# Splitting 128x128 fp32 transposes into two 64-row tiles in a streaming encoder step

## The chip, the cores and the metric

The kernel runs on one core of a Trainium2 chip. The metric is device time in microseconds (us) from launch to end; a verdict on a changed kernel comes from timed runs of both kernels on the same chip. The engines of the core are TensorE (in the profile PE for matmuls and PEld for the loads of stationary operands), VectorE (DVE), ScalarE (ACT), GpSimd (POOL) and SyncE (SP, which issues transfers).

## The reference: what is computed

One inference step of a one-layer encoder, for a prompt of 512 frames and a sample of 32 frames of a running stream, in fp32. The input (model width 1024) is normalised and projected by one wide matrix. Two branches follow:

- an mLSTM branch: causal convolution and silu, four heads of width 512 with queries, keys and values, a gated score matrix, a matrix memory, a layer norm per head;
- an HGRN2 branch: eight heads of width 128 with a gated, decaying linear attention, an RMS norm per head and a silu gate.

```python
hm = _head_layernorm(hm.transpose(0, 2, 1, 3), mnorm_g[l].astype(f32))
hm = (hm + m_skip[l].astype(f32) * c) * jax.nn.silu(z_m.astype(f32))
ya = hm.astype(x.dtype) @ w_brm[l]
...
oh = _head_rmsnorm(oh.transpose(0, 2, 1, 3), hnorm_g[l].astype(f32)) * jax.nn.silu(g_h.astype(f32))
yb = oh.astype(x.dtype) @ w_brh[l]
y = jax.nn.sigmoid(ga) * ya + jax.nn.sigmoid(gb) * yb
h = h + y @ w_out[l]
h = h + jax.nn.sigmoid(h @ w_pg[l]) * (p[l] @ w_ple[l])
```

The branches are merged, projected, gated with a per-layer embedding and normalised. Outputs are both streams and all new states (convolution rows, memories, normalisers).

## The kernel before

All activations lie with channels on the 128 partitions and the 544 = 32 + 512 frames along the free dimension. Dense products are written as three products of a high and a low part (fp32r operands), as in `dense` (line 160) and in the classes `One` (line 420) and `Two` (line 477), whose matmuls are lines 460 and 608. `Two` computes two output tiles with seven products of half-size blocks and is the main part of the TensorE work. Such a product's matmul has 272 moving columns.

A `Pump` (line 702) holds the projections still to be done. The attention work of a head is a Python generator: `mchain(h, pump)` for the mLSTM, `chain(h)` (line 1801) for HGRN2. Each `yield n` hands TensorE over to the pump for n half steps, so that the head's own work stands between projection matmuls. TensorE's order is thus written out by hand (`tc.manual_schedule` with the engine PE), and the other engines' order comes from a planner with priorities (`tc.high_priority`) and from `tc.issue_after`. PSUM tiles of the head's work come from `paux` (line 101): two banks of 512 fp32 each, two such tiles in turn; the projections have four single banks from another pool.

Where a head needs another layout, TensorE transposes: `PE.transpose(out, in_, identity)` is a matmul whose stationary operand is the data and whose moving operand is an identity matrix. The places, with the tiles' names in the profile:

- `kt` (line 1122): keys of a head, four blocks of 128 frames, four transposes each; ScalarE then writes the weighted high part (line 1126), VectorE the low part (line 1127). `kts` (line 1135) is the same for the sample, three copies of 32 columns.
- `vt` and `vts` (lines 1157, 1175): the values of heads 1 to 3, with copies in lines 1164, 1165, 1178 and 1182.
- `yt` (lines 1307, 1308): the head's output back to channels on partitions, four blocks of the prompt and one of the sample, for each of four channel tiles per head; VectorE adds it to the skip path in lines 1314 and 1315.
- `pd` (line 1871): five transposes per HGRN2 head, summed along the free dimension by one reduction (line 1873).
- `ht` (lines 1902, 1903): values and keys of a HGRN2 head, five transposes each; ScalarE copies them (lines 1905 to 1909).
- `hoT` (lines 1975, 1976): the HGRN2 head's output, partly with the anti-diagonal `anti` in place of `ident` to turn the order of frames; VectorE multiplies it with the norm's gain and the gate (lines 1979, 1980). The gate itself is made in line 1749.

Other matmuls that use part of the array's rows or columns are the column transposes `cols` (line 916, 4 rows), the broadcasts of the norm (line 248, in part 32 or 16 rows), and the sample's products `nm` (line 1203) and `vq` (line 1586), which have 32 stationary columns.

Of the kernel before, what the change touches and what calls it, by code (L numbers as in the profile page):

```python
# [9 lines left out]
F32 = mybir.dt.float32  # L10
# [16 lines left out]
KH = HD // P  # L27
HH = 8
NB = NP // P
# [7 lines left out]
QUADS = P // NS  # L37
# [25 lines left out]
V_FG, V_CW, V_CB, V_MG, V_SK, V_LB, V_HG, V_CS, V_GV = 0, 8, 72, 88, 104, 120, 136, 144, 192  # L63
# [4 lines left out]
def hybrid_step(ctx: ExitStack, tc: tile.TileContext, a, o):  # L68
    nc = tc.nc
    V, S, G, PE = nc.vector, nc.scalar, nc.gpsimd, nc.tensor  # L70
# [20 lines left out]
    def two(ap):  # L91
        return ap.rearrange("p (a b) -> p a b", a=2)
# [129 lines left out]
    def vcol(i):  # L222
        return vec[:, i : i + 1]
# [888 lines left out]
    def mchain(h, pump):  # L1112
# [5 lines left out]
        for b in range(NB):  # L1118
            yield 4 if h else 1
            pt = paux(f"kt{h}{b}")  # L1120
            for f in range(KH):
                PE.transpose(pt[:, 0, f * P : (f + 1) * P], kf[f][:, NS + b * P : NS + (b + 1) * P], ident)  # L1122
            kh, kl = slot(f"kwh{h}{b}", F32R), slot(f"kwl{h}{b}", F32R)
            wc = col[:, 10 + b, h : h + 1]
            with tc.high_priority():
                kh_ = S.mul(kh[:, :HD], pt[:, 0, :], wc)
                kl_ = V.scalar_tensor_tensor(kl[:, :HD], pt[:, 0, :], wc, kh[:, :HD].bitcast(F32), ALU.mult, ALU.subtract)
            kw.append((kh, kl))
            if h == 0 and b == NB - 2:
                with tc.issue_after(kh_.ins), tc.issue_after(kl_.ins):  # L1130
                    sample_values(vsum)
        yield 4 if h else 2
        pt = paux(f"kts{h}")
        for f in range(KH):
            PE.transpose(pt[: 3 * NS, 0, f * P : (f + 1) * P], ksm[:, f], ident)

        kws = small("kws", [3 * NS, HD], F32R, bufs=1)
        wc = cols[:, 1, h : h + 1]
        with tc.high_priority():
            S.mul(kws, pt[: 3 * NS, 0, :], wc)  # L1140
            lo = slice(2 * NS, 3 * NS)
            low = V.scalar_tensor_tensor(kws[lo], pt[lo, 0, :], wc[lo], kws[lo].bitcast(F32), ALU.mult, ALU.subtract)
# [4 lines left out]
        if h == 0:  # L1147
            vv, vs = t["vv"], t["vs"]
        else:
            yield max(0, max(pump.when["v", f] for f in range(KH)) - pump.done)  # L1150
            vt = t["vt"]
            vv = []
            for b in range(NB):
                yield 1
                pt = paux(f"vt{h}{b}")
                for f in range(KH):
                    PE.transpose(pt[:, 0, f * P : (f + 1) * P], vt[f][:, NS + b * P : NS + (b + 1) * P], ident)
                if b < 2:
                    vhl = sp.tile([P, 2, SLOT], F32R, tag="d", name=f"vhl{h}{b}", bufs=2)
                    vh, vl = vhl[:, 0], vhl[:, 1]  # L1160
                else:
                    vh, vl = slot(f"vh{h}{b}", F32R), slot(f"vl{h}{b}", F32R)
                with tc.high_priority():
                    S.copy(vh[:, :HD], pt[:, 0, :])
                    V.tensor_tensor(vl[:, :HD], pt[:, 0, :], vh[:, :HD].bitcast(F32), ALU.subtract)
                G.tensor_copy(vh[:, HD:VW], one4)
                filled = G.tensor_copy(vl[:, HD:VW], zero4)
                vv.append((vh, vl))
            yield 1
            pt = paux(f"vts{h}")  # L1170
            vsm, copied = triple(vt, "vsm", t["copied"])
            with tc.issue_after(filled.ins):
                make_late(3 if h < MH - 1 else 2, copied)
            for f in range(KH):
                PE.transpose(pt[: 3 * NS, 0, f * P : (f + 1) * P], vsm[:, f], ident)
            vs = small("vs", [3 * NS, VW], F32R, bufs=1)
            with tc.high_priority():
                S.copy(vs[:, :HD], pt[: 3 * NS, 0, :])
            G.tensor_copy(vs[:, HD:VW], vone)
            lo = slice(NS, 2 * NS)  # L1180
            with tc.high_priority():
                low = V.tensor_tensor(vs[lo, :HD], pt[lo, 0, :], vs[lo, :HD].bitcast(F32), ALU.subtract)
        yield 3

        def new_memory(f, g):
# [113 lines left out]
        for f in range(KH):  # L1299
            while parts:  # L1300
                yield 4
                new_memory(*parts.pop(0))
            yield max(GAP - (16 if h == MH - 1 else 0 if h else 4) if f == 0 else 1 if h else 2, pump.when["z", f] - pump.done)
            ft = h * KH + f
            pt = paux(f"yt{ft}")
            for b in range(NB):
                PE.transpose(pt[:, 0, b * P : (b + 1) * P], yb[b][:, f * P : (f + 1) * P], ident)
# [388 lines left out]
    def units():  # L1696
# [104 lines left out]
    def chain(h):  # L1801
# [10 lines left out]
        for li, c in enumerate(LEVELS):  # L1812
# [53 lines left out]
            if li == 0:  # L1866

                yield 1
                pn = paux(f"pd{h}")
                for b, c_ in enumerate([c_ for c_, _, _ in chunks] + [slice(NA, NA + P)]):  # L1870
                    PE.transpose(pn[:, b // NB, b % NB * P : (b % NB + 1) * P], kq[:, c_], ident)
                with tc.high_priority():
                    V.tensor_reduce(
                        dg, pn.rearrange("p a t -> p (a t)")[:, : 5 * P].rearrange("p (b t) -> p b t", t=P), AX.X, ALU.add
                    )
            if li == (4 if h < HH - 1 else 6) and h:
                yield 1
                finish(h - 1)
# [19 lines left out]
        for n, src, dst, dss in ((0, ii, it, its), (2, kk, kt, kts)):  # L1898
            yield n
            pt = paux(f"ht{h}")  # L1900
            for b, (c, _, _) in enumerate(chunks):
                PE.transpose(pt[:, 0, b * P : (b + 1) * P], src[:, c], ident)  # L1902
            PE.transpose(pt[:, 1, :P], quads(src, n // 2), ident)
            with tc.high_priority():
                S.copy(dst, pt[:, 0, :])
                if n:
                    S.mul(dss, pt[:, 1, :P], 1.0 / QUADS)
                else:
                    S.copy(dss, pt[:, 1, :P])
# [60 lines left out]
    def finish(h):  # L1970

        ov, osb, gg = (hs[h][k] for k in ("ov", "osb", "gg"))
        pt = paux(f"hoT{h}")
        for b, (_, _, j) in enumerate(chunks):
            PE.transpose(pt[:, 0, b * P : (b + 1) * P], ov[:, b * P : (b + 1) * P], ident if j else anti)
        PE.transpose(pt[:, 1, :P], osb, anti)
        g = vcol(V_HG + h)
        ob = slot(f"ob{h}")
        V.scalar_tensor_tensor(ob[:, NS:T], pt[:, 0, :], g, gg[:, NS:T], ALU.mult, ALU.mult)
# [315 lines left out]
```

## Time and profile before

| | |
|---|---|
| timed runs, median of 3 | 1104.29 us |
| lowest and highest | 1103.76 and 1106.26 us |
| profiled execution, first to last instruction (span) | 1101.5 us |
| TensorE matmul, busy | 1092.4 us |
| VectorE, busy | 922.8 us |
| ScalarE, busy | 693.1 us |
| GpSimd, busy | 209.5 us |

The profiled execution's own time is known as its span alone, 1101.5 us; the median of the timed runs is 2.8 us longer. In the views below a row names the line of the kernel, the engine, the operation, the tiles as out<-in, and shapes as partitions x elements; for matmuls rows\*columns of the stationary operand stands ahead. A matmul's shown length includes the depth of its pipeline, so the distance of two starts tells its rate, not its length. In the rows of a timeline the first column is the start, the second the length of a group of like instructions, and xN their count.

### The profile page before, as it was taken

What the parts mean: (1) busy time and instruction counts of PE and PEld (TensorE: products, weight loads), DVE (VectorE), ACT (ScalarE), POOL (GpSimd) and SP (SyncE); (2) the same over time, 40 slices, a digit from 0 to 9 for tenths busy, and PEclk for the clock granted to TensorE, in tenths of its full rate; (3) what the DMA queues carried; (4) which work ended last, traced back from release to release, by engine and by line L of the source; (5) the groups of instructions that cost most, each with busy time, mean ns of one, the idle gap of its engine ahead of it and who ended that gap; (6) DMA issues with size and microseconds to landing.
All of it is one profiled execution on the core that took longest, in us unless ns stands there. A gap on an engine that the chain in (4) does not pass through costs nothing.

```text
span 1101.5 us, 23773 instructions
## 1 busy us (share of the span) xinstructions
PE 1092.4 (99%) x8625; PEld 1070.9 (97%) x8625; DVE 922.8 (84%) x2103; ACT 693.1 (63%) x1579; POOL 209.5 (19%) x375
## 2 busy tenths in 40 slices
PE   9999999999999999999999999999999999999997
PEld 9899999999999999999999999999999999999997
DVE  7889988686896786986888799999999977778885
ACT  7777557754666554665656476776776666446683
POOL 5204010303022021202120123232232210000002
PEclk9999999999999999999999999999999999999999
DMA  7135415639355276554798665666765683337753
GB/s 241 50 124 157 156 58 185 158 125 220 119 178 179 93 178 176 164 167 146 212 261 254 172 145 141 144 135 152 159 145 150 155 222 103 110 90 242 247 180 121
DMA packets 97262, 176.58 MB, mean 160 GB/s; under 512 B 11284, under 2 KB 18580, under 8 KB 96888
## 3 DMA queue, kind: packets, MB, share of 16 engines
q1 hardware_dynamic: 81072, 141.01, 39.9%
q0 software_dynamic: 15184, 32.93, 16.2%
q8 instruction: 68, 1.11, 0.4%
q10 hardware_dynamic: 888, 1.12, 0.3%
q14 instruction: 50, 0.41, 0.1%
HBM read 150.10 MB, written 41.69 MB: 174 GB/s over the span
## 4 chain that ended last, share of the span: by engine, by line
PE 93%; DMA 3%; DVE 2%; issue 1%; SPq 0%; ACT 0%; POOL 0%; ACTq 0%; POOLq 0%
PE d L608 44%; PE ya L167 9%; PE yb L167 4%; PE q L167 4%; PE k L167 4%; PE C L1077 4%; PE nm L1257 3%; PE sc L1037 2%; PE pl L1832 2%; PE u L291 2%; PE d L460 2%; PE vp L1576 2%; DMA ws<-in_w_in 1%; PE ple L167 1%; PE kt L1122 1%; PE ht L1902 1%
## 5 line engine op out<-in xcount | busy, mean ns | idle before, releaser
L495 POOL DMA_DIRECT2D ws<-in_w_in x46 | 40.2, 875 | 211.3 <-DVE hkq L1850 32.2
L622 ACT COPY t<-d 128x272 f32<-128x272 f32 x153 | 58.0, 379 | 14.0 <-PE d L608 14.0
L1850 DVE TENSOR_TENSOR hkq<-hkq,q 128x288 f32<-128x288 f32 (+1 forms) x96 | 40.7, 431 | 2.6 <-PE pl L1834 1.0
L785 DVE SCALAR_TENSOR_TENSOR cv<-ub,vec,cv 128x547 f32<-128x547 f32 x48 | 37.6, 784 | 1.6 <-ACT cv L780 1.2
L1832 PE MATMUL pl<-hkq,km 128*128 128x128 f32 x224 | 36.2, 283 | 0.6 <-ACT km L1818 0.5
L1818 ACT COPY km<-hkq 128x256 f32<-128x256 f32 x56 | 23.9, 428 | 14.2 <-DVE hkq L1850 5.2
L1832 PEld LDWEIGHTS pl<-hkq,km 128*128 128x128 f32 x224 | 30.3, 189 | 2.0 <-ACT km L1818 1.5
L1191 DVE SCALAR_TENSOR_TENSOR c<-c,wi,Cs 128x258 f32<-128x258 f32 x32 | 15.3, 479 | 18.8 <-PE Cs L1189 18.5
L1354 DVE TENSOR_TENSOR y<-ya,y 128x272 f32<-128x272 f32 x48 | 18.9, 435 | 12.1 <-PE ya L167 10.3
L1089 ACT COPY Co<-C 128x258 f32<-128x258 f32 x30 | 9.8, 378 | 27.3 <-PE C L1077 24.9
L1857 DVE COPY_PREDICATED at<-lmask,pl 128x256 f32<-128x256 uint8 (+1 forms) x56 | 25.2, 451 | 0.1
L777 POOL COPY uo<-ub 128x3 f32<-128x3 f32 x16 | 18.7, 1167 | 34.5 <-DVE ub L631 26.6
L1268 ACT COPY y<-nm 128x516 f32<-128x516 f32 x16 | 9.4, 590 | 23.0 <-PE nm L1257 22.5
L133 POOL TENSOR_TENSOR wple50l<-wple5r,wple50h 128x256 fp32r<-128x256 f32 x1 | 0.7, 736 | 120.9 <-ACT wple50h L132 120.9
L961 POOL COPY ksm<-kf 128x96 f32<-128x96 f32 x16 | 7.1, 445 | 84.9 <-ACT kf L975 84.9
L961 POOL COPY vsm<-vt 128x96 f32<-128x96 f32 x12 | 6.3, 525 | 85.9 <-ACT vt L633 43.5
L1797 POOL TENSOR_SCALAR_AFFINE_SELECT aa<-at 128x128 f32<-128x128 f32 x32 | 19.6, 643 | 8.2 <-DVE at L1857 8.0
L581 POOL DMA_DIRECT2D ws<-in_w_in x14 | 14.6, 1043 | 33.1 <-DVE ws272l L133 27.3
L1245 DVE BATCH_NORM_STATS2 bs<-y 128x6 f32<-128x512 f32 (+1 forms) x20 | 13.8, 692 | 8.3 <-ACT y L1268 8.0
L1257 PE MATMUL nm<-vhl,sh 128*128 128x258 f32 x112 | 18.4, 286 | 0.0
L376 POOL DMA_DIRECT2D w_pg_d<-in_w_pg x16 | 13.1, 818 | 25.1 <-issue 21.4
L1956 ACT ACTIVATE osq<-kq 128x128 f32<-128x128 f32 x32 | 9.8, 305 | 12.4 <-DVE kq L1951 12.1
(4735 smaller groups left out, 5086.7 us busy)
## 6 DMA issues: line engine op xcount, KB each, us to landing
ws<-in_w_in POOLq DMA_DIRECT2D x60, 256.0 KB, 4.9
ws<-in_w_in SPq DMA_DIRECT2D x46, 256.0 KB, 3.9
ya_d<-y SPq DMA_DIRECT2D x32, 272.0 KB, 2.3
y<-ya_d SPq DMA_DIRECT2D x24, 272.0 KB, 3.3
w_out_d<-in_w_out POOLq DMA_DIRECT2D x24, 256.0 KB, 6.5
w_pg_d<-in_w_pg POOLq DMA_DIRECT2D x24, 256.0 KB, 6.5
c<-in_C SPq DMA_DIRECT2D x16, 258.0 KB, 3.8
out_Cs<-c SPq DMA_DIRECT2D x16, 258.0 KB, 3.8
```

Source lines behind the costliest of these rows:

```text
L167: PE.matmul(both[b][:m, :TH], part(w, off + k * step, m, x), xx[:, half(b)], start=(k == 0 and j == 0), stop=(k == n - 1 and j == 2),)
L291: PE.matmul(both[b][:m, :TH], part(w, off + k * step, m, x), xx[:, half(b)], start=(k == 0 and j == 0), stop=(k == KD - 1 and j == 2),)
L495: G.dma_start(t, piece(u, i), accum_op=ALU.add)
L608: PE.matmul(ps, ww[:, c], xx, start=(start and k == 0 and j == 0), stop=end, skip_group_check=not start,)
L622: self.kept = S.copy(t, ps)
L785: V.scalar_tensor_tensor(cv[:, :547], ub[:, j : j + 547], vcol(V_CW + 4 * ft + j), cv[:, :547], ALU.mult, ALU.add)
L1077: PE.matmul(pn[g][:, :VH], kw[b][x][:, f * P : (f + 1) * P], vv[b][y][:, g * VH : (g + 1) * VH], start=(b == 0 and j == 0), stop=(b == NB ...
L1257: PE.matmul(pn[:, g, :VH], st[j][x][:, (i - j) * P : (i - j + 1) * P], vv[j][y][:, g * VH : (g + 1) * VH], start=(j == 0 and q == 0), stop ...
L1818: low = S.copy(km.rearrange("p (n j c) -> p n j c", j=2, c=c), view(kk, HB, ((2 * c, NA // (2 * c)), (c - HB, 2), (1, c))),)
L1832: PE.matmul(out, km[:, b * P : (b + 1) * P], view(qq, b * P, dims), start=True, stop=True)
L1850: V.tensor_tensor(x, x, d, ALU.mult)
L1857: V.copy_predicated(at[:, :n], lmask[:, li, :n], pn[:, 0, :n])
```

## The change

Every 128x128 transpose becomes two: the first takes the upper 64 rows of the stationary operand (partitions 0 to 63) with a 64x64 piece of the identity, the second the lower 64 rows. Each moves 64 columns, and each writes its 64 result columns into its own PSUM bank of the tile. A transposed block thus lies half in bank 0 and half in bank 1, and all readers go through views (`turned` for the PSUM side, `quarters` for the SBUF side) that put the halves back in order. With kt and kts, yt and hoT, one VectorE instruction becomes two, over half the columns each. The sample parts of yt and hoT become single transposes of 32 rows and 32 moving columns in bank 0. In HGRN2 the norm's gain is multiplied into the gate instead of into the transposed output.

```diff
+    HP = P // 2
+
+    def turn(pt, i, src, eye=None):
+
+        n = src.shape[-1]
+        for r in range(2):
+            k = slice(r * HP, (r + 1) * HP)
+            at_ = ident[k, k] if eye is None else eye[k, P - (r + 1) * HP : P - r * HP]
+            PE.transpose(pt[:n, r, i * HP : (i + 1) * HP], src[k], at_)
+
+    def turned(pt, n, m=P):
+        return pt[:m, :, : n * HP].rearrange("p r (f c) -> p f r c", f=n)
+
+    def quarters(t):
+        return t.rearrange("p (f r c) -> p f r c", r=2, c=HP)
...
-                PE.transpose(pt[:, 0, f * P : (f + 1) * P], kf[f][:, NS + b * P : NS + (b + 1) * P], ident)
+                turn(pt, f, kf[f][:, NS + b * P : NS + (b + 1) * P])
...
-                kh_ = S.mul(kh[:, :HD], pt[:, 0, :], wc)
-                kl_ = V.scalar_tensor_tensor(kl[:, :HD], pt[:, 0, :], wc, kh[:, :HD].bitcast(F32), ALU.mult, ALU.subtract)
+                rows, hi, lo = turned(pt, KH), quarters(kh[:, :HD]), quarters(kl[:, :HD])
+                kh_ = S.mul(hi, rows, wc)
+                for r in range(2):
+                    kl_ = V.scalar_tensor_tensor(
+                        lo[:, :, r], rows[:, :, r], wc, hi[:, :, r].bitcast(F32), ALU.mult, ALU.subtract
+                    )
...
-                PE.transpose(pt[:, 0, b * P : (b + 1) * P], yb[b][:, f * P : (f + 1) * P], ident)
-            PE.transpose(pt[:, 1, :P], yb[NB][:, f * P : (f + 1) * P], ident)
+                turn(pt, b, yb[b][:, f * P : (f + 1) * P])
+            PE.transpose(pt[:, 0, 2 * P : 2 * P + NS], yb[NB][:NS, f * P : (f + 1) * P], ident[:NS, :NS])
...
-                V.scalar_tensor_tensor(c[:, NS:T], pt[:, 0, :], g, c[:, NS:T], ALU.mult, ALU.add)
-                V.scalar_tensor_tensor(c[:, :NS], pt[:, 1, :NS], g, c[:, :NS], ALU.mult, ALU.add)
+                for r in range(2):
+                    cr = quarters(c[:, NS:T])[:, :, r]
+                    V.scalar_tensor_tensor(cr, turned(pt, NB)[:, :, r], g, cr, ALU.mult, ALU.add)
+                V.scalar_tensor_tensor(c[:, :NS], pt[:, 0, 2 * P : 2 * P + NS], g, c[:, :NS], ALU.mult, ALU.add)
...
-            V.tensor_tensor(t[:, :T], t[:, :T], sg[:, :T], ALU.mult)
+            V.scalar_tensor_tensor(t[:, :T], t[:, :T], vcol(V_HG + h), sg[:, :T], ALU.mult, ALU.mult)
...
-                PE.transpose(pt[:, 0, b * P : (b + 1) * P], src[:, c], ident)
-            PE.transpose(pt[:, 1, :P], quads(src, n // 2), ident)
+                turn(pt, b, src[:, c])
+            turn(pt, NB, quads(src, n // 2))
...
-            PE.transpose(pt[:, 0, b * P : (b + 1) * P], ov[:, b * P : (b + 1) * P], ident if j else anti)
-        PE.transpose(pt[:, 1, :P], osb, anti)
+            turn(pt, b, ov[:, b * P : (b + 1) * P], None if j else anti)
+        PE.transpose(pt[:, 0, 2 * P : 2 * P + NS], osb[:NS], anti[:NS, P - NS :])
...
-        V.scalar_tensor_tensor(ob[:, NS:T], pt[:, 0, :], g, gg[:, NS:T], ALU.mult, ALU.mult)
-        V.scalar_tensor_tensor(ob[:, :NS], pt[:, 1, P - NS : P], g, gg[:, :NS], ALU.mult, ALU.mult)
+        V.tensor_tensor(oq[:, :2], rows[:, :2, ::-1], gq[:, :2], ALU.mult)
+        V.tensor_tensor(oq[:, 2:], rows[:, 2:], gq[:, 2:], ALU.mult)
+        V.tensor_tensor(ob[:, :NS], pt[:, 0, 2 * P : 2 * P + NS], gg[:, :NS], ALU.mult)
```

The other places (kts, vt, vts and pd) are rewritten in the same way.

More of the change, by code (lines that the diff above doesn't have):

```diff
@@ L1134, in mchain @@
         for f in range(KH):
-            PE.transpose(pt[: 3 * NS, 0, f * P : (f + 1) * P], ksm[:, f], ident)
+            turn(pt, f, ksm[:, f])
         kws = small("kws", [3 * NS, HD], F32R, bufs=1)
@@ L1139, in mchain @@
         with tc.high_priority():
-            S.mul(kws, pt[: 3 * NS, 0, :], wc)
+            rows, kq = turned(pt, KH, 3 * NS), quarters(kws)
+            S.mul(kq, rows, wc)
             lo = slice(2 * NS, 3 * NS)
-            low = V.scalar_tensor_tensor(kws[lo], pt[lo, 0, :], wc[lo], kws[lo].bitcast(F32), ALU.mult, ALU.subtract)
+            for r in range(2):
+                low = V.scalar_tensor_tensor(
+                    kq[lo, :, r], rows[lo, :, r], wc[lo], kq[lo, :, r].bitcast(F32), ALU.mult, ALU.subtract
+                )
         c0 = [eslot(f"c0{h}{f}") for f in range(KH)]
@@ L1156, in mchain @@
                 for f in range(KH):
-                    PE.transpose(pt[:, 0, f * P : (f + 1) * P], vt[f][:, NS + b * P : NS + (b + 1) * P], ident)
+                    turn(pt, f, vt[f][:, NS + b * P : NS + (b + 1) * P])
                 if b < 2:
@@ L1174, in mchain @@
             for f in range(KH):
-                PE.transpose(pt[: 3 * NS, 0, f * P : (f + 1) * P], vsm[:, f], ident)
+                turn(pt, f, vsm[:, f])
             vs = small("vs", [3 * NS, VW], F32R, bufs=1)
             with tc.high_priority():
-                S.copy(vs[:, :HD], pt[: 3 * NS, 0, :])
+                S.copy(quarters(vs[:, :HD]), turned(pt, KH, 3 * NS))
             G.tensor_copy(vs[:, HD:VW], vone)
@@ L1313, in mchain @@
             with tc.high_priority():
[L1314 to L1315 removed]
+                for r in range(2):
+                    cr = quarters(c[:, NS:T])[:, :, r]
+                    V.scalar_tensor_tensor(cr, turned(pt, NB)[:, :, r], g, cr, ALU.mult, ALU.add)
+                V.scalar_tensor_tensor(c[:, :NS], pt[:, 0, 2 * P : 2 * P + NS], g, c[:, :NS], ALU.mult, ALU.add)
             with nullcontext() if 0 < h < MH - 1 else tc.high_priority():
@@ L1870, in chain @@
                 for b, c_ in enumerate([c_ for c_, _, _ in chunks] + [slice(NA, NA + P)]):
-                    PE.transpose(pn[:, b // NB, b % NB * P : (b % NB + 1) * P], kq[:, c_], ident)
+                    turn(pn, b, kq[:, c_])
                 with tc.high_priority():
-                    V.tensor_reduce(
-                        dg, pn.rearrange("p a t -> p (a t)")[:, : 5 * P].rearrange("p (b t) -> p b t", t=P), AX.X, ALU.add
-                    )
+                    V.tensor_reduce(dg, turned(pn, NB + 1), AX.XY, ALU.add)
             if li == (4 if h < HH - 1 else 6) and h:
```

22 lines of the change are left out of this document (15 added, 7 removed).

## The prediction

> **What bounds the kernel now.** The page is read first, for the engine that sets the span: its head, the busy times, the granted clock, and the chain of work that ended last, by engine.
>
> ```profile
> span 1101.5 us, 23773 instructions
> ...
> PE 1092.4 (99%) x8625; PEld 1070.9 (97%) x8625; DVE 922.8 (84%) x2103; ACT 693.1 (63%) x1579; POOL 209.5 (19%) x375
> ...
> PEclk9999999999999999999999999999999999999999
> ...
> PE 93%; DMA 3%; DVE 2%; issue 1%; SPq 0%; ACT 0%; POOL 0%; ACTq 0%; POOLq 0%
> ```
>
> Then the busy times by stretch: the mLSTM heads are 100 to 600 us, the HGRN2 heads 600 to 870 us.
>
> ```profile
> 100.00:600.00 500.00, 499.45 (x3979) 490.11 (x3978) 401.60 (x862) 300.33 (x639) 90.41 (x184) 1.00 0.58 169
> 600.00:870.00 270.00, 269.33 (x2182) 266.66 (x2181) 255.72 (x690) 184.57 (x502) 70.18 (x101) 1.00 0.64 151
> ```
>
> TensorE stands still for 0.55 us of the first stretch and 0.67 us of the second, at full clock. Whatever TensorE time the change adds or removes there goes to the end one for one. VectorE has 98.4 us free in the first stretch, but only 14.3 us in the second.
>
> The transposes, all in these stretches, by line (duration min/median/max; it includes pipeline depth, so it isn't the rate):
>
> ```profile
> L1122 PE MATMUL kt<-ident,kf x64: 270/272/328, 109.1 to 534.5; 128*128 128x128 f32 x64
> L1135 PE MATMUL kts<-ident,ksm x16: 270/272/273, 115.0 to 538.0; 128*96 128x128 f32 x16
> L1157 PE MATMUL vt<-ident,vt x48: 270/272/316, 250.3 to 550.3; 128*128 128x128 f32 x48
> L1175 PE MATMUL vts<-ident,vsm x12: 272/273/286, 255.2 to 551.6; 128*96 128x128 f32 x12
> L1307 PE MATMUL yt<-ident,y x64: 270/272/300, 153.6 to 584.5; 128*128 128x128 f32 x64
> L1871 PE MATMUL pd<-ident,kq x40: 270/272/273, 629.0 to 843.3; 128*128 128x128 f32 x40
> L1902 PE MATMUL ht<-ident,hi x32: 270/272/299, 647.4 to 862.4; 128*128 128x128 f32 x32
> L1975 PE MATMUL hoT<-anti,kq x16: 270/272/273, 672.4 to 883.0; 128*128 128x128 f32 x16
> ```
>
> They come in short runs between the projections' matmuls: 35 runs of four (kt 16, kts 4, vt 12, vts 3) and 48 of five (yt 16 with line 1308, pd 8, ht 16 with line 1903 and a second source, hoT 8 with line 1976 and ident rows). That is 140 + 240 = 380 transposes; 356 are split and 24 (lines 1308 and 1976) become small 32-row ones.
>
> **What a run costs now.** The first run of kt in order of time, matmuls (PE) and then weight loads (PEld); columns are start, length of the group, count:
>
> ```profile
> 108.89 0.42 PE L460 MATMUL d<-xh,wi340l 128*128 128x272 f32 x2
> 109.15 0.60 PE L1122 MATMUL kt<-ident,kf 128*128 128x128 f32 x4
> 109.50 0.50 PE L460 MATMUL d<-xh,wi340h 128*128 128x272 f32 x2
> ...
> 114.97 0.60 PE L1135 MATMUL kts<-ident,ksm 128*96 128x128 f32 x4
> ```
>
> ```profile
> 109.03 0.48 PEld L1122 LDWEIGHTS kt<-ident,kf 128*128 128x128 f32 x4
> 109.48 0.30 PEld L460 LDWEIGHTS d<-xh,wi340h 128*128 128x128 f32 x2
> 109.72 0.32 PEld L460 LDWEIGHTS d<-xl,wi340h 128*128 128x128 f32 x2
> 109.97 0.19 PEld L460 LDWEIGHTS d<-xh,wi340l 128*128 128x128 f32 x1
> ```
>
> Less the last one's 0.272, kt's group puts its fourth start at 109.48: three steps in 0.33 us, 0.109 each. kts, with 96 weight columns instead of 128, takes the same 0.60 us, so the step is the 128 moving columns (0.85 ns each), with the weight load hidden. The load of the first transpose is issued at 109.03, 0.01 us after the preceding matmul's start (108.89 + 0.42 - 0.29 = 109.02): nothing drains. Behind the run d starts early on paper and slips; its second matmul starts at 109.50 + 0.50 - 0.29 = 109.71, so the first one counts from 109.71 - 0.125 = 109.585, where 0.125 is the step of the loads 109.72 to 109.97 halved. From d to d a run of four takes 0.57 us, one of five 0.68.
>
> **What a change of tile height costs.** The kernel has this already, in two places: 32-row matmuls between 128-row ones. First the small column transposes (4 rows, so in the array's 32-row tiles, and the same kind of fp32 transpose):
>
> ```profile
> 90.73 0.42 PE L167 MATMUL q<-cs3h,wq001l 128*128 128x272 f32 x2
> 91.08 1.19 PEld L916 LDWEIGHTS cols<-ident,row 4*128 4x128 f32 x18 [0.15 <-issue]
> 92.19 0.22 PEld L918 LDWEIGHTS cols<-ident,r 4*96 4x96 f32 x3
> 92.22 0.28 PE L918 MATMUL cols<-ident,r 4*96 4x4 f32 x3
> 92.43 0.52 PE L167 MATMUL q<-cs0h,wq010h 128*128 128x272 f32 x2
> ```
>
> Second, the broadcast of the norm, full-height rows and then one block of 32 rows:
>
> ```profile
> 25.93 0.50 PE L248 MATMUL r0pb<-ident,rms_r 128*128 128x128 f32 x3
> ...
> 26.35 0.29 PEld L248 LDWEIGHTS r0pb<-ident,rms_r 32*128 32x128 f32 x2
> 26.68 0.30 PEld L291 LDWEIGHTS u<-x,wu30h 128*128 128x128 f32 x2
> ```
>
> Going in: the last q starts at 90.73 + 0.42 - 0.29 = 90.86 and streams about 0.115; the load of cols comes at 91.08, some 0.10 after that, where kt's came 0.01 after the start. In the broadcast the last full-height matmul starts at 26.155, streams 128 columns in 0.109, and the 32-row load comes at 26.35, 0.09 later. No work stands between. Going out: the last cols matmul starts at 92.32 and the load of q comes at 92.43, 0.11 later; that load's matmul counts from 92.43 + 0.52 - 0.29 - 0.125 = 92.53. So each switch empties the array, about 0.09 us, and the next load, otherwise hidden, stands open: 0.107 for a plain one (92.53 less 92.43; d's two behind kt are 0.30 - 0.19 = 0.11 apart), and about 0.056 for a transpose, since 18 loads of 128 columns in cols take (1.19 - 0.14) / 17 = 0.062 each, and of 96 columns (0.22 - 0.12) / 2 = 0.05, that is 0.44 ns a column and 0.006.
>
> **The change, part by part.** *A pair of half-height tiles.* Each has a load of 128 columns, 0.062, and 64 moving columns, 0.054. If both tiles work side by side, a pair takes the longer, 0.062; one after the other, 0.124. No two row tiles are at work in the trace; nearest is a row where four column tiles are:
>
> ```profile
> 119.05 0.16 PEld L1203 LDWEIGHTS nm<-c,qw 128*32 128x32 f32 x8
> ```
>
> Eight loads of 32 columns are through within 0.16 us; at the plain load's 0.84 ns a column (0.107 / 128) they would take 0.215 in turn. So loads of different tiles overlap; I take 0.062, saving 0.047 per pair, and keep 0.124 for the range.
>
> *The switch in:* the preceding d streams 0.115, drains 0.095, the first load is open for 0.056: 0.266 from d to the first pair, where it is 109.15 - 109.02 = 0.13 now: +0.137. *The switch out:* last pair 0.054, drain 0.09, d's load 0.107: 0.251, where it is 0.57 - 0.13 - 3 x 0.109 = 0.115 now: +0.136. Between them three steps of 0.062 instead of 0.109: -0.142. Run of four: +0.131. Run of five pairs (pd, ht): +0.083. With 96 columns (kts, vts) a pair takes about 0.057 and the first load 0.042: +0.096.
>
> *yt and hoT* end with a 32-row tile, a second switch inside the run: from the last pair to it 0.054 + 0.09 + 0.056 = 0.200 instead of 0.109, and out of it 0.027 + 0.09 + 0.107 = 0.224 instead of 0.115. With +0.137 and -0.142 this makes +0.194.
>
> Sum on TensorE: 28 x 0.131 + 7 x 0.096 + 24 x 0.083 + 24 x 0.194 = 3.7 + 0.7 + 2.0 + 4.7 = **11.0 us** (3.5 of it in the HGRN2 heads).
>
> Weighed against a page: the four-row loads ran at 0.062 for 128 columns. The Trainium skill, TensorE: Matmul & The Clock Gate, section LDWEIGHTS, gives columns / 1.2 whatever the row count, so 0.107. By it a pair would be no shorter than a whole transpose, and the sum that of the first rival's lower end. The transposes' rows contradict it; q's plain load agrees.
>
> *VectorE.* Two halves replace one scalar_tensor_tensor of 512 columns in kt, kts and yt:
>
> ```profile
> L1127 DVE SCALAR_TENSOR_TENSOR kwl<-kt,col,kwh x16: 737/744/753, 110.9 to 535.7; 128x512 fp32r<-128x512 f32 x16
> L1191 DVE SCALAR_TENSOR_TENSOR c<-c,wi,Cs 128x258 f32<-128x258 f32 x32 | 15.3, 479 | 18.8 <-PE Cs L1189 18.5
> L1979 DVE SCALAR_TENSOR_TENSOR ob<-hoT,vec,hg x8: 739/751/752, 674.1 to 884.2; 128x512 f32<-128x512 f32 x8
> L1850 DVE TENSOR_TENSOR hkq<-hkq,q 128x256 f32<-128x256 f32 x64 | 26.9, 420 | 1.3 <-PE pl L1832 0.5
> ```
>
> 2 x 0.479 - 0.744 = 0.21, for 36 of them 7.7 us, before 600 us, where 98 are free. In hoT 2 x 0.42 - 0.751 = 0.09, 0.7 us in all, and the gate's scale moves into a multiply as long as before or a little longer; the HGRN2 heads' 14.3 us cover this, and TensorE's own 3.5 us add to the cover. ScalarE's copies keep their count and size; no row shows what reading two banks by turns costs, but even a microsecond more for each of the 51 would fit into the 200 and 85 us that ScalarE has free in the two stretches. The cover ends where transposes come close together: the first head's kt runs are 1.2 us apart on two buffers, and one there already waits for the VectorE part. I put 0.4 us for that and for weight splits that come later; bounds 0 and 2. No DMA and no wait on another queue is added or moved.
>
> Total: 1101.5 + 11.0 + 0.4 = 1112.9 us of span. The median of the timed runs stands 2.8 us over the profiled span (1104.29 - 1101.5), so **1115.7 us**.
>
> **Rivals.** *Tiles take turns (slower still).* If the two loads share their path, a pair costs 0.124: +0.378 for four, +0.393 for five, +0.442 for yt and hoT, about 0.29 with 96 columns: 32.6 us. If only the streams take turns, a pair costs 0.109, the run +0.318 or so, with +0.38 for yt and hoT: 27.8 us. Time 1132 to 1137. Against it stand the column tiles' overlapping loads; for it, that those use different columns and here both tiles fill the same ones.
>
> *No emptying between 64- and 128-row tiles (faster).* Then the first load hides behind d as now, d's behind the last pair, and every pair saves 0.047: 356 x 0.047 + 24 x 0.047 = 17.9 us, less 0.4: 1087. It decides if a switch, in and out together, costs less than 3 x 0.047 = 0.14 us. For it: the trace has 32-row switches only. Against it: both kinds of matmul pay there, at each of the four edges shown. The same skill page, Part 3, says that a load is pulled ahead of matmuls in flight if its row group differs; a load for all rows after a 64-row tile has no such free group.
>
> *Half of it.* Only one side of a switch empties the array: the 0.273 of a run falls to about 0.14, what the pairs save: -7 to 0 us, 1097 to 1105.
>
> **How the numbers follow.** The forecast, drains with side-by-side tiles, has 0.58, own range 1112 to 1119 (a pair of 0.056 to 0.07, drains of 0.08 to 0.1, VectorE's 0 to 2 us). Tiles taking turns 0.22, no emptying 0.12, half 0.08. The range of 1103 to 1137 reaches over the upper rival to its bound and leaves out the faster one and part of the half. What this kernel's measurement can tell from no change is about 0.2%, 2.2 us. Faster: 0.12 and 0.03 of the half, 0.15. Same: 0.05 of the half. Slower: 0.80.
>
> **What will show it.** Right: before each run of kt the first load about 0.2 us after the last d's start, not 0.01; d's load 0.14 us behind the last pair; pairs 0.06 apart; TensorE still 99% busy and the span longer in both stretches, with yt and hoT worst. Pairs 0.11 or more apart mean the first rival; first loads that start with the d before them mean the second. I'm wrong altogether if TensorE gets idle time released by VectorE or ScalarE of more than 3 us.

## The result, and the profile after

The changed kernel takes 1113.9 us, median of four runs (1112.96 to 1114.45), beside 1104.03 us for the kernel before on the same chip: ratio 1.0086, 95% interval 1.0071 to 1.0100. It is slower by 9.9 us. The forecast was 1115.7, with 1112 to 1119 as its own range.

The page of the changed kernel, its head and the busy times by engine:

```profile
span 1111.7 us, 24543 instructions
...
PE 1102.7 (99%) x8981; PEld 1064.0 (96%) x8981; DVE 929.2 (84%) x2147; ACT 694.4 (62%) x1579; POOL 203.6 (18%) x375
```

The span grew by 10.2 us and TensorE's busy time by 10.3 (1102.7 less 1092.4). TensorE stands still no longer than before, 9.0 us against 9.1. Busy here is a modelled time: a matmul counts until its result is through, so an array that is being emptied counts as busy (below, the d ahead of kt counts until 108.97 + 0.41 = 109.38, past kt's first start at 109.32). The weight loads show it: there are 356 more of them, their busy time is 6.9 us less (1064.0 against 1070.9), and the load path stands idle for 47.7 us instead of 30.6. The Trainium skill, Perfetto Trace Analysis, section Identifying the Most-Contended Engine, calls the matmul row's busy share no good measure of how close TensorE is to its roofline, and names the busy share of the weight loads, beside the floating-point work done, to use instead. Here the first stayed at 99%, and the second fell from 97% to 96%.

By stretch, in the same columns as the table of before (TensorE, loads, VectorE, ScalarE, GpSimd, clock, DMA share, GB/s):

```profile
100.00:600.00 500.00, 498.56 (x4114) 477.97 (x4113) 401.75 (x887) 293.79 (x627) 81.80 (x184) 1.00 0.57 164
600.00:870.00 270.00, 269.45 (x2297) 261.73 (x2296) 251.45 (x686) 184.99 (x494) 68.78 (x95) 1.00 0.64 155
```

TensorE is idle for 1.44 us of the first stretch (0.55 before) and 0.55 of the second (0.67 before). So with VectorE's 44 further instructions it stands idle for less than a microsecond more, on balance.

The same run of kt as in the prediction, matmuls and then loads of the changed kernel:

```profile
108.97 0.41 PE L476 MATMUL d<-xh,wi340l 128*128 128x272 f32 x2
109.32 0.46 PE L128 MATMUL kt<-ident,kf 64*128 64x64 f32 x8
109.71 0.51 PE L476 MATMUL d<-xh,wi340h 128*128 128x272 f32 x2
```

```profile
109.31 0.33 PEld L128 LDWEIGHTS kt<-ident,kf 64*128 64x128 f32 x8
109.71 0.30 PEld L476 LDWEIGHTS d<-xh,wi340h 128*128 128x128 f32 x2
109.94 0.31 PEld L476 LDWEIGHTS d<-xl,wi340h 128*128 128x128 f32 x2
```

Read as in the prediction: the last d before the run starts at 108.97 + 0.41 - 0.29 = 109.09, and the first load comes 0.22 us later, where it came 0.01 later before. The eight loads span 0.33 us with one load's own 0.13 in it, so three steps from pair to pair take 0.20, 0.067 each by these rounded rows; instruction by instruction the two loads of a pair start 3 to 4 ns apart, and the pairs 0.059 to 0.062. The last pair's matmul starts about 109.71 - 0.15, and the first d behind the run counts from 109.71 + 0.51 - 0.29 - 0.125 = 109.805. From d to d the run takes 0.715 us; it took 0.57.

In the HGRN2 heads, a run of five pairs (pd) and one with a 32-row tile (hoT):

```profile
638.24 0.28 PE L624 MATMUL d<-xfh,ws249l 128*128 128x272 f32 x1
638.46 0.53 PE L128 MATMUL pd<-ident,kq 64*128 64x64 f32 x10
...
639.15 0.28 PE L624 MATMUL d<-xfl,ws249h 128*128 128x272 f32 x1
...
681.65 0.28 PE L624 MATMUL d<-xh,ws450l 128*128 128x272 f32 x1
681.87 0.34 PE L128 MATMUL hoT<-anti,kq 64*128 64x64 f32 x4
682.04 0.29 PE L128 MATMUL hoT<-ident,kq 64*128 64x64 f32 x4
682.26 0.24 PE L2008 MATMUL hoT<-anti,osb 32*128 32x32 f32 x1
...
682.66 0.29 PE L624 MATMUL d<-xfl,ws274h 128*128 128x272 f32 x1
```

Counted from the second d behind the run, less a step of 0.125, pd's run is 639.15 - 0.125 - 638.24 = 0.785 us and hoT's 682.66 - 0.125 - 681.65 = 0.885. Medians from d to d over all runs of a kind, in us:

| run | before | after | difference | the prediction's |
| --- | --- | --- | --- | --- |
| kt (16) | 0.567 | 0.716 | +0.150 | +0.131 |
| vt (12) | 0.570 | 0.715 | +0.146 | +0.131 |
| kts (4) | 0.564 | 0.683 | +0.119 | +0.096 |
| vts (3) | 0.616 | 0.675 | +0.059 | +0.096 |
| pd (8) | 0.679 | 0.780 | +0.101 | +0.083 |
| ht (16) | 0.672 | 0.776 | +0.104 | +0.083 |
| yt (16) | 0.674 | 0.888 | +0.214 | +0.194 |
| hoT (8) | 0.674 | 0.886 | +0.212 | +0.194 |

Each kind of run is a little dearer than forecast, but for vts, whose runs already held a wait before (0.616 us, where those of kt and kts take 0.567 and 0.564). With all other matmuls of the two traces laid side by side in their order, and each run counted with the three matmuls behind it, 10.8 us of the difference arise at the transposes' runs and 0.4 us elsewhere. So the last matmul comes 11.3 us later. The span grew by 10.2 only, because what follows the last matmul happened to be 1.0 us shorter (5.8 us instead of 6.8; it lies between 5.6 and 7.2 in all traces of this case). The medians alone would give some 12.5; the rest went into waits inside or near the runs that were there already. The third run of kt in the kernel before is such a one: it starts 0.43 us after the d before it where 0.26 is usual, and in the changed kernel its wait is gone: it starts 0.35 us after its d, as the first run does.

```profile
111.29 0.41 PE L460 MATMUL d<-xh,wi341l 128*128 128x272 f32 x2
111.72 0.66 PE L1122 MATMUL kt<-ident,kf 128*128 128x128 f32 x4
```

```profile
111.66 0.41 PE L476 MATMUL d<-xh,wi341l 128*128 128x272 f32 x2
112.01 0.46 PE L128 MATMUL kt<-ident,kf 64*128 64x64 f32 x8
```

### The profile page after: what moved, and what is told of

Read it like the earlier page. It is cut to its first block, busy times and chain, and to the rows that moved or that the text cites. A ratio compares the mean times of both kernels' runs of the same rounds, so it can differ in the third digit from the quotient of the medians.

```text
span 1111.7 us, 24543 instructions
## 1 busy us (share of the span) xinstructions
PE 1102.7 (99%) x8981; PEld 1064.0 (96%) x8981; DVE 929.2 (84%) x2147; ACT 694.4 (62%) x1579; POOL 203.6 (18%) x375
## 4 chain that ended last, share of the span: by engine, by line
PE 91%; DVE 3%; DMA 3%; ACT 2%; issue 1%; POOL 0%; SPq 0%; ACTq 0%; DVEq 0%
PE d L624 42%; PE ya L183 9%; PE yb L183 4%; PE q L183 4%; PE k L183 4%; PE C L1093 4%; PE nm L1288 3%; PE sc L1053 2%; PE d L476 2%; PE pl L1865 2%; PE u L307 2%; PE vp L1609 2%; PE ple L183 1%; DMA ws<-in_w_in 1%; DMA ww_pg1r<-w_pg_d 1%
## 5 line engine op out<-in xcount | busy, mean ns | idle before, releaser
L597 POOL DMA_DIRECT2D ws<-in_w_in x14 | 14.3, 1023 | 35.9 <-DVE ws272l L149 29.3
L1276 DVE BATCH_NORM_STATS2 bs<-y 128x6 f32<-128x512 f32 (+1 forms) x20 | 13.8, 692 | 8.1 <-ACT y L1299 7.8
L793 POOL COPY uo<-ub 128x3 f32<-128x3 f32 x16 | 10.1, 629 | 42.8 <-DVE ub L647 29.4
```

## The experiments

Ratios are against the kernel before, run on the same chip beside each. The theory is the prediction's: a run of half-height tiles empties the array at both ends (a fixed price), and each pair, its two tiles side by side, gives 0.047 us back. The rivals: the two tiles take turns; the readers on VectorE, not TensorE, set the price; the price is one per transpose, not one per run.

**Both tiles on the same rows.** The two tiles of each pair are put on the upper 64 rows, so that they can't be at work together. The kernel leaves out the lower rows.

```
-            at_ = ident[k, k] if eye is None else eye[k, P - (r + 1) * HP : P - r * HP]
-            PE.transpose(pt[:n, r, i * HP : (i + 1) * HP], src[k], at_)
+            at_, top = (ident if eye is None else eye)[:HP, ...], src[:HP]
+            PE.transpose(pt[:n, r, i * HP : (i + 1) * HP], top, at_)
```

> The changed kernel, but both tiles of a pair take the upper 64 rows (the lower rows aren't transposed at all, so this part of the computation is left out); number, shape and readers of the instructions are the same. Theory (the two tiles of a pair work side by side because their rows differ): now they take turns, a pair costs 0.124 instead of 0.062, 356 x 0.062 = 22 us more than the changed kernel, 1136, ratio to before 1.029. Rival (they take turns already, and the changed kernel's loss is that): no change, 1113.9.

Measured: 1133.87 us, ratio 1.0265 (1.0244 to 1.0285). The same run of kt, its loads and the d behind it:

```profile
109.53 0.57 PEld L129 LDWEIGHTS kt<-ident,kf 64*128 64x128 f32 x8 [0.15 <-DVE dss L1082]
110.17 0.30 PEld L477 LDWEIGHTS d<-xh,wi340h 128*128 128x128 f32 x2
```

Eight loads now span 0.57 us: less one load's 0.13, seven steps of 0.063 in turn. The run takes 0.961 us from d to d, 0.245 more than in the changed kernel (0.248 was forecast). So in the change the two tiles of a pair do work side by side, and the upper end of the prediction's first rival is what taking turns would have cost: this kernel is 20 us slower than the changed one, and the prediction's sum for that rival was 32.6 us over the kernel before, where by the ratio 29.3 were measured.

**One half-height tile added, and one whole transpose added.** Two kernels, both the kernel before with one more transpose at the end of the 35 runs of kt, kts, vt and vts, into a bank that these leave unused: a single 64-row tile in the one, a whole transpose in the other.

```
+    def extra(pt, src):
+        k = slice(0, 64)
+        PE.transpose(pt[: src.shape[-1], 1, 0:64], src[k], ident[k, k])
...
+            extra(pt, kf[0][:, NS + b * P : NS + (b + 1) * P])
```

```
+    def extra(pt, src):
+        PE.transpose(pt[: src.shape[-1], 1, :P], src, ident)
```

> The kernel before, with one more transpose of a 64-row tile at the end of each of the 35 runs of kt, kts, vt and vts, into the unused bank, read by nobody. Theory: each adds a switch in and out: 0.109 + 0.09 + 0.056 + 0.054 + 0.09 + 0.107 = 0.506 from the last whole transpose to d instead of 0.115, +0.39 us, 35 times 13.7: 1117.7, ratio 1.0124. Rival (no emptying; a half-height tile only costs its own work of 0.06): 2 us, 1106.

> As the run with one more tile, but the added transpose is whole, 128 rows. Both theories: 35 x 0.109 = 3.8 us more than before, 1107.8, ratio 1.0035. By the theory of the switch the bigger transpose is thus 10 us cheaper than the smaller one; by the rival it is dearer.

Measured: with the half-height tile 1118.93 us, ratio 1.0125 (1.0108 to 1.0142); with the whole one 1108.38 us, ratio 1.0033 (1.0021 to 1.0045). By the ratios that is 13.8 and 3.6 us: half the work costs nearly four times as much. The run of kt with the half-height tile, matmuls and loads:

```profile
109.62 0.60 PE L1126 MATMUL kt<-ident,kf 128*128 128x128 f32 x4
110.16 0.27 PE L122 MATMUL kt<-ident,kf 64*128 64x64 f32 x1
110.36 0.52 PE L464 MATMUL d<-xh,wi340h 128*128 128x272 f32 x2
```

```profile
110.15 0.13 PEld L122 LDWEIGHTS kt<-ident,kf 64*128 64x128 f32 x1 [0.17 <-issue]
110.36 0.30 PEld L464 LDWEIGHTS d<-xh,wi340h 128*128 128x128 f32 x2
```

The last whole transpose starts at 109.62 + 0.60 - 0.27 = 109.95 and streams 0.109; the tile's load comes at 110.15, 0.09 after that. The tile itself is open and short (0.056 and 0.054), and d's load comes at 110.36, 0.10 after 110.15 + 0.11 = 110.26. So there is one emptying of 0.09 to 0.10 us at each edge, between 128-row and 64-row tiles as between 128-row and 32-row ones, and nothing but TensorE's own order stands at those places ("issue", with nothing waited for). This is what the prediction's rivals of no emptying, and of emptying on one side only, denied. The run is 0.398 us longer than before, forecast 0.39; with the whole transpose 0.11.

**Only pd and ht split.** The kernel before, with 24 of its 83 runs in halves: the runs of five pairs, whose readers (one reduction, and ScalarE's copies) need no further instruction of VectorE.

```
-                    PE.transpose(pn[:, b // NB, b % NB * P : (b % NB + 1) * P], kq[:, c_], ident)
+                    turn(pn, b, kq[:, c_])
...
-                PE.transpose(pt[:, 0, b * P : (b + 1) * P], src[:, c], ident)
-            PE.transpose(pt[:, 1, :P], quads(src, n // 2), ident)
+                turn(pt, b, src[:, c])
+            turn(pt, NB, quads(src, n // 2))
```

> The kernel before with pd and ht alone split (24 runs of five pairs), no VectorE instruction more than before. Theory: 24 x 0.104 = 2.5 us by what the changed kernel's runs of pd and ht showed, 1106.8, ratio 1.0023. Rival (the readers): 1104.3, ratio 1.000.

Measured: 1106.67 us, ratio 1.0021 (1.0012 to 1.0030): 2.3 us for 24 runs, 0.10 each, which is what their medians show in the changed kernel.

**Twelve in a run.** The 35 runs of kt, kts, vt and vts are lengthened from four to twelve, once in the kernel before and once in the changed one.

```
+            for f in [*range(KH)] * 2:
+                PE.transpose(pt[:, 1, f * P : (f + 1) * P], kf[f][:, NS + b * P : NS + (b + 1) * P], ident)
```

```
+            for f in [*range(KH)] * 2:
+                turn(pt, KH + f, kf[f][:, NS + b * P : NS + (b + 1) * P])
```

> The kernel before, with each of the 35 runs of kt, kts, vt and vts lengthened from four whole transposes to twelve (the eight more go into the bank that these runs leave unused; nobody reads them). Both theories: a step of 0.109 us each, so kt's run 0.567 + 8 x 0.109 = 1.44 us from d to d, and 35 x 0.872 = 30.5 us in all: 1134.5 us, ratio 1.0276. It is the yardstick for the same runs in halves.

> The changed kernel, with the same 35 runs lengthened from four pairs of half-height tiles to twelve (into columns of both banks that nobody reads). My theory (a fixed price for the two switches, about 0.30 us a run, against 0.047 saved by each pair after the first): kt's run 0.716 + 8 x 0.061 = 1.20 us, shorter than the 1.44 of twelve whole ones, and 35 x 0.49 = 17.1 us over the changed kernel: 1131.0 us, ratio 1.0244; so 3.5 us faster than twelve whole ones, although the other 48 runs are still split and with four a run the split lost 9.8 us. Rival (the split costs the same per transpose, whatever the length of the run): kt's run 1.44 x 0.716 / 0.567 = 1.82 us, 1152 us, ratio 1.043.

Measured: whole 1132.88 us, ratio 1.0260 (1.0245 to 1.0275); in pairs 1133.95 us (1131.11 to 1135.83), ratio 1.0260 (1.0241 to 1.0278). The run of kt with twelve whole transposes, then with twelve pairs:

```profile
109.03 0.42 PE L460 MATMUL d<-xh,wi340l 128*128 128x272 f32 x2
109.29 0.60 PE L1122 MATMUL kt<-ident,kf 128*128 128x128 f32 x4
109.72 1.04 PE L1124 MATMUL kt<-ident,kf 128*128 128x128 f32 x8
110.52 0.50 PE L460 MATMUL d<-xh,wi340h 128*128 128x272 f32 x2
```

```profile
109.33 0.41 PE L476 MATMUL d<-xh,wi340l 128*128 128x272 f32 x2
109.67 0.96 PE L128 MATMUL kt<-ident,kf 64*128 64x64 f32 x24
110.56 0.52 PE L476 MATMUL d<-xh,wi340h 128*128 128x272 f32 x2
```

From d to d: 110.52 + 0.50 - 0.29 - 0.125 - 109.16 = 1.445 us whole, and 110.56 + 0.52 - 0.29 - 0.125 - 109.45 = 1.215 in pairs (medians 1.442 and 1.217; forecast 1.44 and 1.20). At four the pairs lose 0.15 us a run, at twelve they win 0.225. The fixed price is therefore shown: the eight further pairs cost 0.063 each, whole ones 0.109, and the two meet after (0.716 - 0.567) / 0.047 = 3.2 more, at about seven in a run.

End to end the 3.5 us of gain that I expected did not appear; the two can't be told apart. TensorE's busy time is only 0.4 us lower with pairs:

```profile
PE 1122.3 (99%) x8905; PEld 1101.2 (97%) x8905; DVE 925.4 (82%) x2103; ACT 695.3 (61%) x1579; POOL 208.8 (18%) x375
```

```profile
PE 1121.9 (99%) x9541; PEld 1082.8 (95%) x9541; DVE 931.3 (82%) x2147; ACT 696.1 (61%) x1579; POOL 199.4 (18%) x375
```

And it stood still for 12.2 us of the 1134.1 in pairs, and for 8.9 of 1131.2 with whole ones. Among the waits of the matmuls with pairs (in all, times, longest) the longest is for a reader:

```profile
PE kt L128 <- DVE kwl L1147: 1.8, 1, 1.8
```

In the first head a run of kt waits 1.8 us for the VectorE part, now two instructions, of an earlier run, which still holds its buffer; with whole transposes that wait is 0.2. This is the place the prediction named as the end of the cover. Laid beside the changed kernel's trace, a lengthened kt run takes 0.50 us more, but the third and the fourth of the first head take 2.5 and 1.2: some 2.6 us of the gain were lost there. Another 2.2 us arose outside the runs, most of it in the HGRN2 heads, where matmuls wait for copies of ScalarE (1.6 us in all, 0.9 with whole transposes).

**The readers alone.** The changed kernel with whole transposes in one bank; the readers of the blocks keep the form that the change gave them, with each scalar_tensor_tensor in two halves.

```
-        for r in range(2):
-            k = slice(r * HP, (r + 1) * HP)
...
-            PE.transpose(pt[:n, r, i * HP : (i + 1) * HP], src[k], at_)
+        b, i = divmod(i, NB)
+        PE.transpose(pt[:n, b, i * P : (i + 1) * P], src, ident if eye is None else eye)
```

> Transposes whole as before, 128 rows into one bank; all readers (ScalarE and VectorE) split as in the change. Theory (the loss is TensorE's changes of tile height): TensorE as before, 1104.0 to 1104.8 us, ratio 1.000 to 1.0007; VectorE some 7 to 9 us busier. Rival (a good part of the 9.9 us is the readers' extra instructions): 1107 or more.

Measured: 1113.8 us, ratio 1.0087 (1.0074 to 1.0101): as slow as the changed kernel, and my expectation was wrong. Taken by its time alone this would have made VectorE the cause. The page of the profile shows another loss: TensorE's busy time is that of the kernel before, and it waits in a place where the changed kernel doesn't.

```profile
PE 1091.1 (98%) x8625; PEld 1069.6 (96%) x8625; DVE 927.9 (83%) x2147; ACT 694.5 (62%) x1579; POOL 204.8 (18%) x375
```

```profile
PE hoT L2006 <- DVE osb L1997: 8.6, 6, 1.4
PE yt L126 <- DVE c L1346: 1.5, 2, 0.7
PE ya L181 <- DVE wbm300l L147: 1.4, 1, 1.4
```

VectorE at that place, first in this kernel and then in the kernel before:

```profile
676.36 0.40 DVE L1892 COPY_PREDICATED at<-lmask,pl 32x32 f32<-32x32 uint8 x2
676.78 0.29 DVE L1997 TENSOR_SCALAR osb<-osb,hr 128x128 f32<-128x128 f32 x1
```

```profile
671.03 0.28 DVE L1967 TENSOR_SCALAR osb<-osb,hr 128x128 f32<-128x128 f32 x1
672.20 0.49 DVE L1857 COPY_PREDICATED at<-lmask,pl 128x288 f32<-128x288 uint8 x1
673.26 0.80 DVE L1861 COPY_PREDICATED at<-lmask,pl 32x32 f32<-32x32 uint8 x4
```

The planner that orders VectorE's work put the scaling of osb behind the predicated copies; in the kernel before it stands ahead of them. What moved it, presumably the other durations of the work before it, wasn't tested. The transpose of osb, which TensorE reaches in its fixed order, then waits up to 1.4 us in six heads. In the changed kernel the scaling is early again and that wait is absent. So the kernel was run a second time with that one instruction given priority:

```
-        V.tensor_scalar(osb, osb, hr[:, NB : NB + 1], None, ALU.mult)
+        with tc.high_priority():
+            V.tensor_scalar(osb, osb, hr[:, NB : NB + 1], None, ALU.mult)
```

> As the run with the readers only (whole transposes, split readers), but the scaling of the sample's output tile osb has priority on VectorE, because in that run the planner had put it behind other work and six hoT runs waited 1.7 us each for it. Theory (switches are the change's loss, the 10 us of the readers-only run are that order): those waits go, what stays is the wait behind the last mLSTM head and in the first head's kt, 1 to 2 us: 1105 to 1106, ratio 1.001 to 1.002. Rival (the readers' extra instructions cost the 10 us by themselves): 1112 or more.

Measured: 1108.36 us, ratio 1.0033 (1.0020 to 1.0045). The wait for osb is gone, and with it some 5.4 us of the median (6 by the ratios). What is left, 3.6 us by the ratio, is dearer than the 1 to 2 us expected. Its stretches:

```profile
100.00:600.00 500.00, 496.28 (x3957) 487.01 (x3956) 404.75 (x896) 298.66 (x636) 82.15 (x185) 1.00 0.58 169
600.00:870.00 270.00, 268.04 (x2168) 265.13 (x2167) 253.45 (x692) 184.44 (x499) 74.50 (x101) 1.00 0.63 149
```

TensorE is idle for 3.72 and 1.96 us, against 0.55 and 0.67 in the kernel before: 4.5 us more. Of its waits those of yt and ya at the end of the last mLSTM head, shown above, are unchanged at 1.5 and 1.4 us, and the matmuls of pl in the HGRN2 heads wait 1.5 us for ScalarE, where it was 0.5. In the changed kernel yt and ya wait 0.6 and 0.4, and pl 0.5. So the two prices, the runs' and the readers', don't add up to the change. That the readers cost less where TensorE itself is late fits this, but no run tests it alone, and none has the priority of osb without the readers' new form.

**The 32-row tile taken back.** The changed kernel, with the sample of yt and hoT transposed whole, behind the pairs.

```
-            PE.transpose(pt[:, 0, 2 * P : 2 * P + NS], yb[NB][:NS, f * P : (f + 1) * P], ident[:NS, :NS])
+            PE.transpose(pt[:, 0, 2 * P : 3 * P], yb[NB][:, f * P : (f + 1) * P], ident)
...
-        PE.transpose(pt[:, 0, 2 * P : 2 * P + NS], osb[:NS], anti[:NS, P - NS :])
+        PE.transpose(pt[:, 0, 2 * P : 3 * P], osb, anti)
```

> The changed kernel, but the sample's transposes of yt and hoT whole (128 rows) at the end of their runs. Theory: one change of height less in 24 runs, and a run ends with 0.20 to the whole transpose and 0.115 out of it: 0.78 us from d to d where the changed kernel has 0.886, so 24 x 0.106 = 2.5 us less, 1111.4, ratio to before 1.0066. Rival (the small tile needs no emptying of its own, since it lies in the upper tile's rows): the whole one is longer by about 0.05 each, 1115.

Measured: 1113.22 us, ratio 1.0088 (1.0074 to 1.0101), no different from the changed kernel, so the 2.5 us expected did not come. The runs are as short as forecast (yt 0.782, hoT 0.777, forecast 0.78, in the changed kernel 0.888 and 0.886), and TensorE's busy time fell by 3.3 us. Its idle time rose by 3.2 (12.2 us, 9.0 in the changed kernel), most of it at the end of the last mLSTM head:

```profile
PE 1099.4 (99%) x8981; PEld 1062.1 (96%) x8981; DVE 929.4 (84%) x2147; ACT 694.0 (62%) x1579; POOL 207.5 (19%) x375
```

```profile
PE yt L128 <- DVE c L1348: 1.9, 3, 0.8
PE ya L183 <- DVE wbm300l L149: 1.8, 1, 1.8
```

The 32-row tile's own price of about 0.11 us a run is shown; that it can be had back at the end of the kernel isn't.

**Ten pairs in one run.** The kernel before, with ht's values and keys in one run instead of two, in halves and whole. Seven being the estimated break-even, ten pairs should have won.

```
-            yield n
+            yield 2 - n
...
-                PE.transpose(pt[:, 0, b * P : (b + 1) * P], src[:, c], ident)
+                turn(pt, b, src[:, c])
```

> The kernel before, but in each HGRN2 head the transposes of values and keys stand in one run of ten, and these alone are split. Theory: one switch in and out for ten pairs; 0.776 + 5 x 0.062 - 0.125 = 0.96 us of TensorE per head instead of 2 x (0.67 - 0.125) = 1.09: 8 x 0.13 = 1.1 us less, 1102.9, ratio 0.999. Rival (a pair saves nothing, only the runs' ends count): 1104 or more.

> The kernel before with the same order (values and keys in one run of ten), not split: tells the order's own cost. Both theories: 1104.0 within 0.5, ratio 0.9995 to 1.0005; ten steps of 0.109.

Measured: in halves 1105.57 us, ratio 1.0008 (0.9999 to 1.0017); whole 1104.69 us, ratio 1.0001 (0.9992 to 1.0010). The first is a miss: its runs aren't compact, and neither are those of the whole one. Loads of the split one, then of the whole one:

```profile
682.13 0.33 PEld L128 LDWEIGHTS ht<-ident,hi 64*128 64x128 f32 x8
682.38 0.14 PEld L128 LDWEIGHTS ht<-ident,snap 64*128 64x128 f32 x2
682.77 0.36 PEld L128 LDWEIGHTS ht<-ident,hkq 64*128 64x128 f32 x8 [0.25 <-PE ht L128]
```

```profile
681.29 0.14 PEld L1903 LDWEIGHTS ht<-ident,snap 128*128 128x128 f32 x1
681.67 0.42 PEld L1902 LDWEIGHTS ht<-ident,hkq 128*128 128x128 f32 x4 [0.24 <-PE ht L1903]
```

The keys' first load stops for 0.33 us behind the values' last pair (682.77 - 682.38 - 0.06), and the run takes 1.43 us, against 1.45 for ten whole transposes. With these the stop is there too, 0.27 us (681.67 - 681.29 - 0.11), so it doesn't come from the height of the tiles. Both rows put some 0.25 us of it down to a matmul of ht itself, the values' last; why the keys wait for that one was not settled, and a compact run of ten in this place wasn't had. The kernels with twelve in a run answered the question instead. None of the versions run beats the kernel before.

## Why the prediction was right

**The bound.** TensorE's time goes to the end one for one: busy time +10.3, span +10.2, median +9.9. Where the two part in these runs (the readers alone, twelve pairs, ten pairs), the rows of TensorE's waits show it.

**Whole transposes.** The step of 0.109 us and the hidden load were read from the trace; a whole transpose added to 35 runs cost 0.11 us a run (in the total 3.6 us, or 0.10).

**A pair.** Taken as 0.062 with both tiles at work; 0.059 to 0.062 in the change, 0.063 in the runs of twelve. The only row for it was that of four column tiles, which is no proof for two row tiles that fill the same columns; the kernel with both tiles on the same rows is. The rule weighed in the prediction (the Trainium skill, TensorE: Matmul & The Clock Gate, section LDWEIGHTS: columns / 1.2, so 0.107 us) doesn't hold for these loads: eight of them in turn took 0.062 each. It holds for the plain loads of d, 0.11 apart.

**The switches.** In: 0.22 us from d's start to the first load, forecast 0.21. Out: d's load 0.15 us behind the last pair, forecast 0.144. The run of four came to 0.716, where the prediction's steps give 0.57 + 0.131 = 0.701. Together the two switches were undersized by about 0.015 us a run, and rounding the runs before up to 0.57 and 0.68 hid a few thousandths more. Going in, only the sum of streaming and drain is measured: the 0.115 for which d was said to stream stands in no row (the starts of its matmuls are 0.125 apart). Going out, and at both edges of the single half-height tile, the drain is 0.09 to 0.10. The argument from row groups that was set against the rival of no emptying carries little: kt's first load takes all 128 rows in the kernel before, and it still starts 0.01 us after the d ahead of it, whose rows are the same. The Trainium skill, TensorEngine Tiling (Array Packing), section Key Properties, says that a change of tiling mode drains TensorE; it gives no price, and the trace's is 0.09 to 0.10 us each way, with the next load open behind it.

**The sum.** 11.0 us forecast at the runs, 10.8 found there; two errors meet in it, the switches' (about +1.3 us) and the waits in and near the runs that the longer runs filled. That they cancel so nearly is luck.

**VectorE.** The halves take 0.477 us where 0.479 was used, and the copies of ScalarE from two banks 0.690 us where one bank took 0.689, so they cost nothing more.

```profile
L1145 DVE SCALAR_TENSOR_TENSOR kwl<-kt,col,kwh 128x256 fp32r<-128x256 f32 x32 | 13.9, 477 | 0.6 <-ACT kwh L1143 0.6
L1143 ACT ACTIVATE kwh<-kt,col 128x512 fp32r<-128x512 f32 x16 | 11.0, 690 | 1.4 <-PE kt L128 1.3
```

The term of 0.4 us stands beside 0.4 us found outside the runs, but this is luck: the 0.4 is what is left of 1.8 us more around the end of the last mLSTM head (570 to 600 us) and of waits that shrank elsewhere, 1.1 us of them in the HGRN2 heads. I placed the term in the first head's kt and in weight splits; in the changed kernel the waits arose for yt (0.6 us) and for ya (0.4), the latter for a split of the head's output. The places named do show in other runs: the first head's kt with twelve pairs, and a weight split (wbm300l, 1.4 to 1.8 us) with the readers alone and with the sample whole. And the free time of a stretch, 98 us of VectorE's in the first, is no cover for an instruction that someone waits for: with whole transposes, and osb early, the same readers cost 3.6 us. What covered them in the change was, as far as these runs tell, TensorE's own delay; the prediction counted that cover for hoT and not for the rest.

**The rest.** The forecast was 1.8 us high, and the matmuls are not where it was: their end was forecast 11.4 us later and came 11.3 later. The span grew by 1.0 less because of what follows the last matmul, and the median stood 2.2 us over the profiled span where 2.8 was taken. Each of the four executions of the changed kernel takes 1.7 to 1.9 us more than its own span, so the 2.8 was in part the draw of one execution.

## What to carry to other kernels

Count the changes of tile height before splitting matmuls into smaller tiles: a run of 64-row tiles between 128-row matmuls pays about 0.10 us of emptying at each end and has the next load open, some 0.29 us in all, against 0.047 us that each pair of fp32 transposes gives back; by that estimate it takes about seven transposes in a row here, and the kernel has runs of four and five. Look at the first load after the switch and not at TensorE's busy share, which counts an emptying array as busy. When an experiment undoes one half of a change, compare the order of the other engines' work before reading its time: here one moved instruction of VectorE cost more than half as much as the whole change.

## What the runs showed of the hardware that was not expected

- A single half-height transpose at the end of a run costs 0.40 us, a whole one 0.11.
- The loads of two 64-row tiles that fill the same 128 columns start 3 to 4 ns apart and run together: 0.06 us for both; on the same rows they follow each other at 0.062 us.
